# The front of a conformer, attention and PEER block: convolution sums in PSUM, projections in another order, part of the attention's elementwise work on ScalarE

## The chip, the cores and the metric

One NeuronCore of a Trainium2 chip runs the whole block as one program. The metric is the device time in microseconds of one execution; it is the median of several runs.

## The reference, cut to what matters

The block has 512 tokens (4 tiles of 128) of width 1024. Its front, which the change is about, is this:

```python
h = rmsnorm(x, norm1_g)
z = h @ w_in                      # 44 column chunks of 128: 16 for the conv, 8 q, 2 k, 2 v, 16 gates
u = z[..., :1024] * sigmoid(z[..., 1024:2048])              # GLU
u = depthwise_conv(u, width 31, centred) + dw_b             # 31 taps, each channel by itself
A = silu(layernorm(u)) @ w_pw
# windowed attention, 16 query heads, 4 key heads, |t-s| <= 128, ALiBi bias, one sink logit per head
p = exp(logits * scale + bias - m); o = (p @ v) / (p.sum() + exp(sink - m))
B = o @ w_o
x = x + (sigmoid(gate_A) * A + sigmoid(gate_B) * B) @ w_out
x = x + PEER(rmsnorm(x)); out = rmsnorm(x)                  # 128x128 experts, 8 heads, top 16
```

## The kernel before

Activations lie transposed: 128 channels on the partitions, 512 tokens along the free axis. Every fp32 product is made of three matmuls on a high and a low half (`mm3`, L61 to L66): L64 is high by high, L65 high by low, L66 low by high. A projection of one 128-column chunk is 8 contraction steps of three matmuls, so 24 matmuls of 128x512 into one PSUM bank (`proj`, L167). Its weights come by one 512 KB DMA of SP (`wraw`, 3 buffers); ACT makes the high half in two pieces (`whi`, L58, 4 buffers), and POOL the low half (`wlo`, L59).

The order of the front in the program text is: norm and transposes; GLU of channel chunks 0 and 1 (`glu`, L191: two projections `pa` and `pg`, a sigmoid on ACT, a product on DVE into `ub`); their convolution on DVE (`conv`, L203: one `TENSOR_SCALAR` for the first tap and 30 `SCALAR_TENSOR_TENSOR` per chunk, the two chunks of a pair taking turns, each adding into the tile `cv` in SBUF); k and v; the distance table; conv of pairs (2, 3), (4, 5) and (6, 7) with the q projections between them; the attention, 4 key groups by 4 query blocks (`attend`, L253); the LayerNorm over `cv`; 16 gate projections (`gate`, L240); then the projections by w_o (L350), w_pw (L388) and w_out, and the PEER part.

One `attend` has, for 4 heads, three score matmuls into a PSUM tile `s`, a DVE reduction that adds the bias and finds the maximum (L267), an exponential on ACT (L275), sums and a reciprocal on DVE, four normalisations on DVE (L282), transposes on PE (`pt`), a split into `ph` (ACT) and `pl` (DVE), and the product with v into `o`.

The order on each engine is not the order of the text. The tile framework schedules ahead of time, by program priority and its own estimates, and each engine then runs its list strictly in that order. What has no dependency on the conv is therefore already spread among its taps. PSUM has 8 banks: before, 2 for `mm` (all projections), 2 for `s`, 2 for `pt`, 1 each for `o` and `ln`.

Of the kernel before, what the change touches and what calls it, by code (L numbers as in the profile page):

```python
# [7 lines left out]
F32 = mybir.dt.float32  # L8
# [4 lines left out]
AF = mybir.ActivationFunctionType  # L13
OP = mybir.AluOpType
AX = mybir.AxisListType
PSUM = bass.MemoryType.PSUM

P = 128
S = 512
D = 1024  # L20
NT = S // P
KD = D // P
TAPS = 31
# [22 lines left out]
def encoder_block(ctx, tc, x, g1, w_in, taps, dwb, lng, lnb, w_pw, sink, w_o, w_out, g2, g2row,  # L46
# [71 lines left out]
    with ExitStack() as fc:  # L118
# [45 lines left out]
            POOL.dma_start(keyt, keys)  # L164
        hT = [(hT_hi[:, k, :], hT_lo[:, k, :]) for k in range(KD)]

        def proj(src, rhs, ws=None, lo_engine=POOL):  # L167
            ws = ws or weights(src, lo_engine)
            ps = psm.tile([P, S], F32, name="mm")
            mm3(ps, ws, rhs)  # L170
            return ps

# [4 lines left out]
        with ExitStack() as ac:  # L177
# [5 lines left out]
            dist = kvp.tile([P, 3 * P], F32, name="dist")  # L183
            aw = ac.enter_context(tc.tile_pool(name="aw", bufs=2))
            psa = ac.enter_context(tc.tile_pool(name="psa", bufs=2, space=PSUM))
            pso = ac.enter_context(tc.tile_pool(name="pso", bufs=1, space=PSUM))

            glup = ExitStack()
            gl = glup.enter_context(tc.tile_pool(name="gl", bufs=2))

            def glu(i):  # L191
                pa = proj(w_in[i], hT, first if i == 0 else None)
                pg = proj(w_in[8 + i], hT)
                sgm = gl.tile([P, S], F32, name="sgm")
                ACT.activation(sgm, pg, AF.Sigmoid)
                ub = gl.tile([P, S + 2 * PAD], F32, name="ub", bufs=4)
                POOL.memset(ub[:, :PAD], 0.0)
                POOL.memset(ub[:, PAD + S:], 0.0)
                with tc.high_priority():
                    DVE.tensor_tensor(ub[:, PAD:PAD + S], pa, sgm, op=OP.mult)  # L200
                return ub

            def conv(pair, ubs):  # L203
                for j in range(TAPS):
                    for i, ub in zip(pair, ubs):
                        acc = cv[:, i, :]
                        if j == 0:
                            DVE.tensor_scalar(acc, ub[:, :S], tapt[:, i, 0:1], vec["dwb"][:, i:i + 1],
                                              op0=OP.mult, op1=OP.add)
                        else:  # L210
                            DVE.scalar_tensor_tensor(acc, ub[:, j:j + S], tapt[:, i, j:j + 1], acc,  # L211
                                                     op0=OP.mult, op1=OP.add)

            conv((0, 1), [glu(0), glu(1)])
            for i in range(2):
                ps = proj(w_in[24 + i], hT)
                with tc.high_priority():
# [22 lines left out]
            def gate(i):  # L240
                ps = proj(w_in[28 + i], hT)
                ACT.activation(sg[i // KD][:, i % KD, :], ps, AF.Copy)
# [3 lines left out]
            def make_bias(g):  # L246
                bt = aw.tile([P, 4, 3 * P], F32, name="bias", bufs=1)
                for i in range(4):
                    slope = 2.0 ** (-8.0 * (4 * g + i + 1) / NH)
                    POOL.tensor_scalar(bt[:, i, :], dist, -8.0 * slope, None, op0=OP.mult)  # L250
                biases[g] = bt

            def attend(g, b):  # L253
                k0, k1 = max(0, b - 1), min(NT, b + 2)
                n = (k1 - k0) * P
                c0 = (k0 - (b - 1)) * P
                rows = slice(64 * (g % 2), 64 * (g % 2) + 64)
                gp = g // 2
                cols = slice(b * P, (b + 1) * P)
                L = aw.tile([P, 4, 3 * P], F32, name="L", bufs=3)  # L260
                m = sm.tile([P, 4], F32, name="m")
                for i in range(4):
                    s_ps = psa.tile([P, S], F32, name="s")
                    mm3(s_ps[:, :n], [(qh[rows, gp * 4 + i, cols], ql[rows, gp * 4 + i, cols])],
                        [(kh[rows, gp, k0 * P:k1 * P], kl[rows, gp, k0 * P:k1 * P])])
                    h = 4 * g + i
                    DVE.tensor_tensor_reduce(L[:, i, :n], s_ps[:, :n], biases[g][:, i, c0:c0 + n], 0.125,  # L267
                                             sinkt[:, h:h + 1], OP.add, OP.max, m[:, i:i + 1])
                nm = sm.tile([P, 4], F32, name="nm")
                DVE.tensor_scalar(nm, m, -1.0, None, op0=OP.mult)  # L270
                es = sm.tile([P, 4], F32, name="es")
                DVE.tensor_tensor(es, sinkt[:, 4 * g:4 * g + 4], m, op=OP.subtract)
                den = sm.tile([P, 4], F32, name="den")
                for i in range(4):
                    ACT.activation(L[:, i, :n], L[:, i, :n], AF.Exp, bias=nm[:, i:i + 1],  # L275
                                   accum_out=den[:, i:i + 1])
                ACT.activation(es, es, AF.Exp)
                DVE.tensor_tensor(den, den, es, op=OP.add)
                rd = sm.tile([P, 4], F32, name="rd")
                DVE.reciprocal(rd, den)  # L280
                for i in range(4):
                    DVE.tensor_scalar(L[:, i, :n], L[:, i, :n], rd[:, i:i + 1], None, op0=OP.mult)  # L282
                o_ps = pso.tile([P, 4, P], F32, name="o")
                for j in range(k1 - k0):
                    pt = psa.tile([P, 4, P], F32, name="pt", bufs=2)
                    for i in range(4):
                        PE.transpose(pt[:, i, :], L[:, i, j * P:(j + 1) * P], ident)
                    ph = aw.tile([P, S], F32R, name="ph")
                    pl = aw.tile([P, S], F32R, name="pl")
                    split(ph, pl, pt.rearrange("p a b -> p (a b)"), DVE)  # L290
                    vcols = slice(gp * P, (gp + 1) * P)
                    mm3(o_ps.rearrange("p a b -> p (a b)"),
                        [(vh[:, k0 + j, vcols], vl[:, k0 + j, vcols])], [(ph, pl)],
                        first=j == 0, last=j == k1 - k0 - 1)
                split(qh[rows, gp * 4:gp * 4 + 4, cols], ql[rows, gp * 4:gp * 4 + 4, cols], o_ps[rows], DVE)
# [5 lines left out]
            DVE.tensor_scalar(dtmp, dist, float(P), 1e32, op0=OP.is_gt, op1=OP.mult)  # L301
            DVE.tensor_tensor(dist, dist, dtmp, op=OP.add)

            conv((2, 3), [glu(2), glu(3)])
            for i in range(4):
                qproj(i)
            conv((4, 5), [glu(4), glu(5)])
            for i in range(4, 8):
                qproj(i)
            conv((6, 7), [glu(6), glu(7)])  # L310
            for g in range(4):
                make_bias(g)
                for b in range(NT):
                    attend(g, b)
            glup.close()
            lnp = ac.enter_context(tc.tile_pool(name="lnp", bufs=2))
            ac_hi, ac_lo = bigtile(), bigtile()
            mu_ps = pso.tile([P, S], F32, name="ln")
# [23 lines left out]
                sgf = sg[i].rearrange("p k s -> p (k s)")  # L342
                ACT.activation(sgf, sgf, AF.Sigmoid)

            for k in range(KD):
                gate(KD + k)
            sigmoid(1)
            for k in range(KD):
                gate(k)
            for j in range(KD):  # L350
                ps = proj(w_o[j], oT, lo_engine=DVE)
                DVE.tensor_tensor(sg[1][:, j, :], ps, sg[1][:, j, :], op=OP.mult)
# [80 lines left out]
    with ExitStack() as rc:  # L433
# [73 lines left out]
        with qc:  # L507
# [45 lines left out]
            for h in range(HP):  # L553
                scs = []
                for p in range(2):
                    n = 2 * h + p
# [251 lines left out]
```

## Time and profile before

| what | value |
|---|---|
| median of 3 runs | 1873.43 us (1873.26 to 1878.59) |
| the profiled execution | 1870.83 us, its span 1869.1 us |
| granted TensorE clock, mean | 0.979 |
| PE, PEld, DVE, ACT, POOL busy | 94%, 80%, 82%, 40%, 56% |
| first projection matmul | 15.57 us |
| conv taps on DVE | 30.5 to 286.3 us |
| first matmul by w_o, first by w_pw | 432.53 us, 477.33 us |

A time is read from the first instruction of the span. "PE busy" counts modelled ends of pipelined matmuls, so a full 20.00 in a 20 us window says only that PE never ran dry; the count of matmuls in a window says how much it did. A fast 128x512 matmul starts 0.227 us after the one before it, about 88 in 20 us.

### The profile page before, as it was taken

What the parts mean: (1) busy time and instruction counts of PE and PEld (TensorE: products, weight loads), DVE (VectorE), ACT (ScalarE), POOL (GpSimd) and SP (SyncE); (2) the same over time, 40 slices, a digit from 0 to 9 for tenths busy, and PEclk for the clock granted to TensorE, in tenths of its full rate; (3) what the DMA queues carried; (4) which work ended last, traced back from release to release, by engine and by line L of the source; (5) the groups of instructions that cost most, each with busy time, mean ns of one, the idle gap of its engine ahead of it and who ended that gap; (6) DMA issues with size and microseconds to landing.
All of it is one profiled execution on the core that took longest, in us unless ns stands there. A gap on an engine that the chain in (4) does not pass through costs nothing.

```text
span 1869.1 us, 25289 instructions
## 1 busy us (share of the span) xinstructions
PE 1751.3 (94%) x8873; PEld 1495.0 (80%) x8873; DVE 1536.5 (82%) x2649; ACT 753.2 (40%) x1329; POOL 1049.0 (56%) x757
## 2 busy tenths in 40 slices
PE   7878879999999986887899999999999999999998
PEld 5656656778887876776889899999999999999886
DVE  5999978854534999999798899998988977797874
ACT  4222325865224414554443333333333333333243
POOL 4544373231015525465535788788887888787611
PEclk9999889999999999999999999999999999999999
DMA  4122111034234202468866989898998888887972
GB/s 152 58 77 75 61 46 35 12 92 167 68 102 150 88 26 93 137 191 253 275 221 239 340 320 337 297 330 317 325 336 306 330 311 316 313 314 292 351 270 97
DMA packets 148943, 379.43 MB, mean 203 GB/s; under 512 B 11520, under 2 KB 63760, under 8 KB 148816
## 3 DMA queue, kind: packets, MB, share of 16 engines
q1 hardware_dynamic: 110832, 241.20, 37.2%
q0 software_dynamic: 37120, 134.52, 20.3%
q10 hardware_dynamic: 864, 2.10, 0.3%
q8 instruction: 69, 1.13, 0.2%
q14 instruction: 58, 0.48, 0.1%
HBM read 346.84 MB, written 30.93 MB: 202 GB/s over the span
## 4 chain that ended last, share of the span: by engine, by line
PE 40%; DVE 14%; DMA 5%; issue 2%; POOL 2%; ACT 1%; SPq 0%; POOLq 0%; DVEq 0%; ACTq 0%
PE acc L65 7%; PE acc L66 7%; PE acc L64 7%; PE hps L66 6%; PE hps L64 6%; PE hps L65 6%; DVE oi L594 1%; DVE ohi L596 1%; DVE olo L597 1%; DVE oj L595 1%; DVE vlo L59 1%; DMA row<-in_v_dram,eidx 1%; DMA vraw<-in_v_dram 1%; DVE ij L496 1%; POOL ulo L59 1%
## 5 line engine op out<-in xcount | busy, mean ns | idle before, releaser
L59 POOL TENSOR_TENSOR ulo<-uraw,uhi 128x512 fp32r<-128x512 f32 x256 | 423.8, 1671 | 279.7 <-ACT uhi L58 262.9
L64 PE MATMUL hps<-big,uhi 128*128 128x384 f32 x1024 | 350.9, 343 | 7.8 <-ACT hb L429 7.7
L66 PE MATMUL hps<-big,ulo 128*128 128x384 f32 x1024 | 350.2, 342 | 2.6 <-POOL ulo L59 2.6
L65 PE MATMUL hps<-big,uhi 128*128 128x384 f32 x1024 | 349.4, 341 | 0.0
L59 POOL TENSOR_TENSOR wlo<-wraw,whi 128x512 fp32r<-128x512 f32 x120 | 194.8, 1631 | 231.5 <-ACT whi L58 205.6
L65 PE MATMUL acc<-vlo,ph 128*128 128x512 f32 x768 | 300.2, 391 | 2.0 <-DVE vlo L59 2.0
L64 PE MATMUL acc<-vhi,ph 128*128 128x512 f32 x768 | 298.9, 390 | 1.2 <-ACT vhi L58 1.2
L66 PE MATMUL acc<-vhi,pl 128*128 128x512 f32 x768 | 299.6, 390 | 0.0
L64 PE MATMUL mm<-big,whi 128*128 128x512 f32 x544 | 224.2, 412 | 28.0 <-DVE ub L200 12.4
L58 ACT ACTIVATE uhi<-uraw 128x512 fp32r<-128x512 f32 x256 | 155.5, 629 | 206.7 <-DMA uraw<-in_ut_dram 83.9
L641 DVE SCALAR_TENSOR_TENSOR yacc<-row,dots,yacc 128x1024 f32<-128x1024 f32 x127 | 189.2, 1490 | 58.0 <-DMA row<-in_v_dram,eidx 57.7
L66 PE MATMUL mm<-big,wlo 128*128 128x512 f32 x544 | 220.2, 405 | 14.5 <-POOL wlo L59 14.4
L630 DVE SCALAR_TENSOR_TENSOR row<-row,h2tok 128x1024 f32<-128x1024 f32 x128 | 193.9, 1521 | 34.6 <-DMA row<-in_u_dram,eidx 33.9
L58 ACT ACTIVATE vhi<-vraw 128x1024 fp32r<-128x1024 f32 x128 | 135.0, 1055 | 212.3 <-DMA vraw<-in_v_dram 200.2
L65 PE MATMUL mm<-big,whi 128*128 128x512 f32 x544 | 220.0, 404 | 0.0
L211 DVE SCALAR_TENSOR_TENSOR cv<-ub,tapt,cv 128x512 f32<-128x512 f32 x240 | 212.1, 930 | 1.8
L58 ACT ACTIVATE whi<-wraw 128x512 fp32r<-128x512 f32 x152 | 94.7, 631 | 287.4 <-PE mm L65 169.7
L64 PEld LDWEIGHTS hps<-big,uhi 128*128 128x128 f32 x1024 | 195.1, 191 | 15.4 <-ACT hb L429 8.7
L623 POOL DMA_INDIRECT row<-in_v_dram,eidx x128 | 176.3, 1377 | 49.3 <-DVE yacc L641 20.3
L623 POOL DMA_INDIRECT row<-in_u_dram,eidx x128 | 182.9, 1429 | 33.1 <-issue 17.5
L65 PEld LDWEIGHTS hps<-big,uhi 128*128 128x128 f32 x1024 | 195.5, 191 | 4.1
L66 PEld LDWEIGHTS hps<-big,ulo 128*128 128x128 f32 x1024 | 194.8, 190 | 3.6 <-POOL ulo L59 3.6
(217 smaller groups left out, 3027.0 us busy)
## 6 DMA issues: line engine op xcount, KB each, us to landing
uraw<-in_ut_dram SPq DMA_DIRECT2D x128, 512.0 KB, 7.1
vraw<-in_v_dram SPq DMA_DIRECT2D x128, 512.0 KB, 5.5
gates_dram<-st SPq DMA_DIRECT2D x12, 2048.0 KB, 9.9
gt<-gates_dram SPq DMA_DIRECT2D x32, 768.0 KB, 7.0
wraw<-in_w_in_dram SPq DMA_DIRECT2D x44, 512.0 KB, 3.3
wraw<-in_w_query_dram SPq DMA_DIRECT2D x16, 512.0 KB, 3.4
oraw<-in_w_out_dram SPq DMA_DIRECT2D x16, 256.0 KB, 3.1
wraw<-in_w_o_dram SPq DMA_DIRECT2D x8, 512.0 KB, 3.8
```

The lines of the kernel that those rows point to most:

```text
L58: ACT.activation(hi, src, AF.Copy)
L59: lo_engine.tensor_tensor(lo, src, f(hi), op=OP.subtract)
L64: PE.matmul(ps, wh, mh, start=first and i == 0, stop=False)
L65: PE.matmul(ps, wh, ml, start=False, stop=False)
L66: PE.matmul(ps, wl, mh, start=False, stop=last and i == n - 1)
L211: DVE.scalar_tensor_tensor(acc, ub[:, j:j + S], tapt[:, i, j:j + 1], acc, op0=OP.mult, op1=OP.add)
L496: DVE.tensor_reduce(ij[t][:, s, hs, :].rearrange("p h k -> p (h k)"), oh.rearrange("p a h k -> p (h k) a"), AX.X, OP.add)
L594: DVE.tensor_tensor(prs(oi), iota8, row(0), op=OP.is_equal)
L595: DVE.tensor_tensor(prs(oj), iota8, row(1), op=OP.is_equal)
L623: POOL.indirect_dma_start(out=row, out_offset=None, in_=table, in_offset=bass.IndirectOffsetOnAxis(ap=eidx[:, c:c + 1], axis=0))
L630: DVE.scalar_tensor_tensor(row, row, 1.0, h2tok, op0=OP.mult, op1=OP.mult, accum_out=dots[:, c:c + 1])
L641: DVE.scalar_tensor_tensor(yacc, row, dots[:, c:c + 1], yacc, op0=OP.mult, op1=OP.add)
```

## The change

Four things are changed. The running sum of the convolution is kept in a PSUM tile (`ca`, two banks, pool `psc`), and only the last tap writes to `cv`. The GLU's two projections use the banks of `s` in place of those of `mm`. The order in the text is another: the GLU chunks 2 and 3 stand ahead of k and v, each later pair's GLU ahead of the conv in front of it, and 3, 6 and 2 of the gate projections stand between the channel pairs, 5 among the attention (`fill`), in the order B, A, B, A. In the attention, the bias tables are made by ACT in place of POOL, and two of each four normalisations by ACT in place of DVE. The banks of `o` and `ln` are opened only after those of `ca` are closed, so no `o` product can start while a conv runs.

```diff
-            pso = ac.enter_context(tc.tile_pool(name="pso", bufs=1, space=PSUM))
             glup = ExitStack()
+            psc = glup.enter_context(tc.tile_pool(name="psc", bufs=2, space=PSUM))
             def glu(i):
-                pa = proj(w_in[i], hT, first if i == 0 else None)
-                pg = proj(w_in[8 + i], hT)
+                pa = proj(w_in[i], hT, first if i == 0 else None, ps=psa.tile([P, S], F32, name="s"))
+                pg = proj(w_in[8 + i], hT, ps=psa.tile([P, S], F32, name="s"))
             def conv(pair, ubs):
+                accs = [psc.tile([P, S], F32, name="ca") for _ in pair]
                 for j in range(TAPS):
-                    for i, ub in zip(pair, ubs):
-                        acc = cv[:, i, :]
+                    for i, ub, acc in zip(pair, ubs, accs):
                         if j == 0:
                             DVE.tensor_scalar(acc, ub[:, :S], ...)
                         else:
-                            DVE.scalar_tensor_tensor(acc, ub[:, j:j + S], tapt[:, i, j:j + 1], acc,
-                                                     op0=OP.mult, op1=OP.add)
+                            DVE.scalar_tensor_tensor(cv[:, i, :] if j == TAPS - 1 else acc, ub[:, j:j + S],
+                                                     tapt[:, i, j:j + 1], acc, op0=OP.mult, op1=OP.add)
-            conv((0, 1), [glu(0), glu(1)])
+            ub01 = [glu(0), glu(1)]
+            conv((0, 1), ub01)
+            ub23 = [glu(2), glu(3)]
...
-                    POOL.tensor_scalar(bt[:, i, :], dist, -8.0 * slope, None, op0=OP.mult)
+                    ACT.activation(bt[:, i, :], dist, AF.Copy, scale=-8.0 * slope)
...
-                    DVE.tensor_scalar(L[:, i, :n], L[:, i, :n], rd[:, i:i + 1], None, op0=OP.mult)
+                    if i % 2:
+                        ACT.activation(L[:, i, :n], L[:, i, :n], AF.Copy, scale=rd[:, i:i + 1])
+                    else:
+                        DVE.tensor_scalar(L[:, i, :n], L[:, i, :n], rd[:, i:i + 1], None, op0=OP.mult)
...
-            conv((2, 3), [glu(2), glu(3)])
+            gates = [gate_of for k in range(KD) for gate_of in (KD + k, k)]
+            def fill(n):
+                for _ in range(n):
+                    gate(gates.pop(0))
             for i in range(4):
                 qproj(i)
-            conv((4, 5), [glu(4), glu(5)])
+            conv((2, 3), ub23)
+            ub45 = [glu(4), glu(5)]
             for i in range(4, 8):
                 qproj(i)
-            conv((6, 7), [glu(6), glu(7)])
+            fill(3)
+            conv((4, 5), ub45)
+            ub67 = [glu(6), glu(7)]
+            fill(6)
+            conv((6, 7), ub67)
+            fill(2)
+            glup.close()
+            pso = ac.enter_context(tc.tile_pool(name="pso", bufs=1, space=PSUM))
             for g in range(4):
                 make_bias(g)
                 for b in range(NT):
                     attend(g, b)
-            glup.close()
+                    if b == 1 or (g, b) == (0, 3):
+                        fill(1)
...
-            for k in range(KD):
-                gate(KD + k)
             sigmoid(1)
-            for k in range(KD):
-                gate(k)
```

Where instructions stand on DVE, in the conv of the second channel pair; `ql` is the low half of a q projection, `L` here a score block of the attention. Before:

```order
L211 SCALAR_TENSOR_TENSOR cv<-ub,tapt,cv 128x512 x8
L59 TENSOR_TENSOR ql<-mm,qh 128x512
L211 SCALAR_TENSOR_TENSOR cv<-ub,tapt,cv 128x512 x13
L267 ISA L,m<-s,bias,sinkt 128x256
L267 ISA m 128x1
L200 TENSOR_TENSOR ub<-mm,sgm 128x512
L211 SCALAR_TENSOR_TENSOR cv<-ub,tapt,cv 128x512
L208 TENSOR_SCALAR cv<-ub,tapt,dwb 128x512
```

And now, at the same q projections:

```order
L210 SCALAR_TENSOR_TENSOR ca<-ub,tapt,ca 128x512 x6
L59 TENSOR_TENSOR ql<-mm,qh 128x512
L210 SCALAR_TENSOR_TENSOR ca<-ub,tapt,ca 128x512 x15
L199 TENSOR_TENSOR ub<-s,sgm 128x512
L210 SCALAR_TENSOR_TENSOR ca<-ub,tapt,ca 128x512 x3
L210 SCALAR_TENSOR_TENSOR cv<-ub,tapt,ca 128x512
L210 SCALAR_TENSOR_TENSOR ca<-ub,tapt,ca 128x512
L207 TENSOR_SCALAR ca<-ub,tapt,dwb 128x512
```

The taps read and write `ca`, and the product that makes `ub` reads the bank `s`. No instruction of the attention stands among the taps now.

On ACT, about the GLU of the last channel pair and the first exponentials (`sgm` is the GLU's sigmoid, `sg` a stored gate, `den` the sum of the exponentials). Before:

```order
L58 ACTIVATE whi<-wraw 128x512 x3
L275 ACT_TABLE_LOAD
L275 ACTIVATE L,den<-L,nm 128x256
L195 ACT_TABLE_LOAD
L195 ACTIVATE sgm<-mm 128x512
L58 ACTIVATE whi<-wraw 128x512
L275 ACT_TABLE_LOAD
L275 ACTIVATE L,den<-L,nm 128x256 x3
L277 ACTIVATE es<-es 128x4
```

And now, behind all GLU sigmoids and eleven of the gates:

```order
L243 ACTIVATE sg_82<-mm 128x512
L58 ACTIVATE whi<-wraw 128x512 x2
L243 ACTIVATE sg_83<-mm 128x512
L276 ACT_TABLE_LOAD
L276 ACTIVATE L,den<-L,nm 128x256 x4
L278 ACTIVATE es<-es 128x4
L276 ACTIVATE L,den<-L,nm 128x384
L284 ACTIVATE L<-L,rd 128x256 x2
```

All eight sigmoids of the GLU and eleven gates come ahead of the first exponential, and each block has two normalisations (L284) on ACT.

On PE, at the end of the attention (`o` is the product with v, `mm<-big` a gate projection, `mm<-qh` one by w_o, `ln<-sq` the LayerNorm's variance). Before:

```order
L64 MATMUL o<-ph,vh 128x512
L65 MATMUL o<-pl,vh 128x512
L66 MATMUL o<-ph,vl 128x512
L65 MATMUL mm<-big,whi 128x512
L66 MATMUL mm<-big,wlo 128x512
L64 MATMUL mm<-big,whi 128x512
```

And now:

```order
L64 MATMUL o<-ph,vh 128x512
L65 MATMUL o<-pl,vh 128x512
L66 MATMUL o<-ph,vl 128x512
L346 MATMUL ln<-sq,ones 128x512 x4
L64 MATMUL mm<-qh,whi 128x512
L65 MATMUL mm<-ql,whi 128x512
L346 MATMUL ln<-sq,ones 128x512 x2
L66 MATMUL mm<-qh,wlo 128x512
```

Before, 113 gate matmuls follow the last `o`; now the variance and then 166 matmuls by w_o follow it, 26 of the 192 by w_o having come earlier.

## Rows read from the trace of the kernel before

**Rows 1.** Windows of 20 us in the conv stretch, all engines.
```profile
core 0: us, PE busy (x) PEld busy (x) DVE busy (x) ACT busy (x) POOL busy (x), PEclk, DMA share, GB/s
40.00:60.00 20.00, 15.13 (x59) 11.79 (x58) 19.82 (x24) 4.61 (x8) 7.36 (x5) 0.88 0.24 81
100.00:120.00 20.00, 13.26 (x51) 10.44 (x50) 19.72 (x25) 3.69 (x7) 6.17 (x4) 0.83 0.17 52
240.00:260.00 20.00, 6.11 (x20) 4.60 (x19) 20.00 (x31) 1.12 (x2) 20.00 (x4) 0.66 0.04 10
```

**Rows 2.** Windows of the conv stretch and of the attention, columns as above.
```profile
280.00:406.00 126.00, 124.63 (x581) 86.88 (x580) 108.05 (x298) 89.57 (x215) 34.48 (x25) 1.00 0.08 27
20.00:262.00 242.00, 197.69 (x786) 152.65 (x786) 231.38 (x292) 59.42 (x102) 124.80 (x75) 0.91 0.20 66
```

**Rows 3.** Waits, 20 to 262 us: total, times, longest.
```profile
PE mm L66 <- POOL wlo L59: 13.9, 1, 13.9
PE mm L64 <- DVE ub L200: 12.4, 4, 6.7
PE mm L64 <- DVE ql L59: 8.0, 5, 3.1
```

**Rows 4.** Conv taps by their line, POOL's low halves by tile: ns min/median/max.
```profile
L211 DVE SCALAR_TENSOR_TENSOR cv<-ub,tapt,cv x240: 733/747/1789, 30.5 to 286.3; 128x512 f32<-128x512 f32 x120
L59 POOL TENSOR_TENSOR wlo<-wraw,whi x88: 1257/1460/21874, 13.0 to 426.2; 128x512 fp32r<-128x512 f32 x88
```

**Rows 5.** Timeline of DVE and POOL: start, length, instruction, count.
```profile
231.34 23.94 DVE L211 SCALAR_TENSOR_TENSOR cv<-ub,tapt,cv 128x512 f32<-128x512 f32 x36
...
234.52 21.87 POOL L59 TENSOR_TENSOR wlo<-wraw,whi 128x512 fp32r<-128x512 f32 x1 [7.74 <-ACT whi L58]
```

**Rows 6.** DVE instructions that read PSUM, and ACT's square into PSUM or SBUF.
```profile
L104 DVE SCALAR_TENSOR_TENSOR big<-mm,g,big x8: 743/747/751, 15.5 to 20.2; 128x512 fp32r<-128x512 f32 x8
...
L59 DVE TENSOR_TENSOR pl<-pt,ph x40: 669/681/692, 255.2 to 405.4; 128x512 fp32r<-128x512 f32 x40
...
L86 ACT ACTIVATE xn<-xt x4: 1040/1049/1058, 6.1 to 10.4; 128x1024 f32<-128x1024 f32 x4
...
L86 ACT ACTIVATE junk<-x x4: 1023/1029/1029, 549.7 to 567.9; 128x1024 f32<-128x1024 f32 x4
```

**Rows 7.** Timeline of PE at three places.
```profile
18.21 0.39 PE L66 MATMUL mm<-big,wlo 128*128 128x512 f32 x1
...
27.75 0.39 PE L66 MATMUL mm<-big,wlo 128*128 128x512 f32 x1
29.18 0.50 PE L64 MATMUL mm<-big,whi 128*128 128x512 f32 x1 [1.04 <-ACT sgm L195]
...
57.00 0.63 PE L65 MATMUL mm<-big,whi 128*128 128x512 f32 x1
...
432.53 0.40 PE L64 MATMUL mm<-qh,whi 128*128 128x512 f32 x1
...
477.33 0.39 PE L64 MATMUL mm<-big,whi 128*128 128x512 f32 x1
```

**Rows 8.** Groups in the attention, 280 to 406 us: busy, mean ns.
```profile
L65 PE MATMUL mm<-big,whi 128*128 128x512 f32 x48 | 21.0, 438 | 0.0
...
L328 PE MATMUL ln<-sq,ones 128*128 128x512 f32 x16 | 8.6, 618 | 0.0
...
L275 ACT ACTIVATE L<-L,nm 128x384 f32<-128x384 f32 x28 | 16.9, 610 | 1.3 <-DVE nm L270 1.1
L275 ACT ACTIVATE L<-L,nm 128x256 f32<-128x256 f32 x28 | 13.9, 501 | 2.0 <-DVE nm L270 1.9
...
L343 ACT ACTIVATE sg<-sg 128x4096 f32<-128x4096 f32 x1 | 3.6, 3625 | 0.0
...
L282 DVE TENSOR_SCALAR L<-L,rd 128x384 f32<-128x384 f32 x32 | 16.1, 553 | 0.1
```

**Rows 9.** LayerNorm's reciprocal, 0 to 600 us: busy, mean ns.
```profile
L331 DVE RECIPROCAL rs<-rs 128x512 f32<-128x512 f32 x1 | 3.4, 3350 | 0.0
```

More of the change, by code (lines that the diff above doesn't have):

```diff
@@ L165, in encoder_block, with proj @@
         hT = [(hT_hi[:, k, :], hT_lo[:, k, :]) for k in range(KD)]
-        def proj(src, rhs, ws=None, lo_engine=POOL):
+        def proj(src, rhs, ws=None, lo_engine=POOL, ps=None):
             ws = ws or weights(src, lo_engine)
-            ps = psm.tile([P, S], F32, name="mm")
+            ps = psm.tile([P, S], F32, name="mm") if ps is None else ps
             mm3(ps, ws, rhs)
```

## The prediction

> **What bounds the kernel now.** I read the windows of the front first, since the change ends there: everything behind the first matmul by w_pw stands as it stood. From 20 to 262 us DVE is busy 231.4 of 242 us [rows 2], and in single windows all of 20.00, while PE does 51 or 59 matmuls where a full window holds 88, and 20 in the window at 240 us [rows 1]. So the conv on DVE sets the pace there and PE waits for it. The waits then say through what: PE waits 13.9 us in one piece for POOL's `wlo`, 12.4 us for the GLU product `ub`, 8.0 us for `ql` [rows 3]. Next, why DVE is that long. A tap takes 747 ns in the median but up to 1789; POOL's low half is 1257 at best and once 21874 [rows 4]. The timeline shows both sides of it: 36 taps run in 23.94 us, 0.665 us each, and in that very stretch one `wlo` of POOL lasts 21.87 us [rows 5]. A tap reads two tensors in SBUF, as does POOL's subtraction; one holds the other up. DVE instructions that read one tensor from PSUM show nothing of it: 40 of `pl` lie between 669 and 692 ns, 8 of L104 between 743 and 751 [rows 6].
>
> The attention is another regime: from 280 to 406 us PE is busy 124.6 of 126 us at clock 1.00, with DVE at 108 and ACT at 90 [rows 2]. There PE is the bound.
>
> The starved PE pays twice: after an idle stretch its matmuls are slower for a while (0.63 us at 57 us, where others show 0.39 [rows 7]), and the mean granted clock of the conv stretch is 0.91, of its worst window 0.66 [rows 1, 2], so for a part of that time it is at the lower of its two levels.
>
> **The change part by part.** PE's work is the same matmuls before and after, so I follow PE's list up to the first matmul by w_pw, which started at 477.33 us [rows 7].
>
> *Stage A, up to the first score.* Now 39 projections stand there: 16 for the GLU, 4 for k and v, 8 q, 11 gates. From 18.21 to 27.75 us lie 42 fast matmuls [rows 7], 0.227 us each, 5.45 us a projection. The first two end at 27.98; the other 37 take 201.7 us. Where two GLU chunks follow each other, the second waits for a bank, 1.2 us at 29.18 [rows 7]; five such places, since k, q and gates use other banks: 6.0 us. The transposes of v add about 1. Stage A ends at 236.7 us, if PE never starves.
>
> Does DVE let it? 240 taps at 0.665 us are 159.6 us; 8 first taps, 8 `ub`, 12 `kl`, `vl`, `ql` and three distance instructions are 18; about 6 go in waits for the first GLU chunks, and DVE starts at 29.2. That is 213 us, and by its list, where 47 taps follow the last `ub` (PE gives it at 193.1 us), about 226. So PE is the bound by some 10 us at the end and 24 in sum; a tap may take up to 0.766 us (53 + 240 times p = 236.7) before PE waits. The `ql` between 6 or 7 taps come every 5.3 us on DVE, just below PE's 5.45. A tap that writes PSUM is not in the trace. From below: `pl`, no scalar operand, 681 ns; from above: a tap that waits out POOL, 1789 ns [rows 4, 6]. L104 is the same instruction with one input in PSUM and takes 747, as the median tap does; and ACT writes 1024 columns to PSUM in 1029 ns and to SBUF in 1049 [rows 6]. I take 0.665 us from start to start. POOL, no longer held up, needs two low halves, 1257 ns each at best [rows 4], in the 5.45 us of a projection.
>
> [...] Here L104 with a PSUM input and the tap without one show 747 ns both. [...]
>
> *Stage B, the attention.* In 280 to 406 us stand 581 records, 144 of them gate matmuls (48 of each of three lines [rows 8]); these are 32.7 us at 0.227, which leaves 93.3 us for 437 of attention and LayerNorm, 0.2135 us each. All 16 blocks have 192 scores, 160 transposes and 120 products with v, and 16 LayerNorm matmuls are recorded twice (x16 for 8 of them [rows 8]): 504 records, 107.6 us. With 5 gates (27.3) and the 26 early matmuls by w_o (6.1) this is 141.0 us. Two things are added: 3 us for the first block, whose chain of scores, exponentials and transposes has only 20 gate matmuls to hide behind, and 3 us for ACT, below. Nothing of it could start earlier, because 8 gates stand in front of it on PE, and DVE does its first score only after the last tap. Stage B ends at 383.7.
>
> ACT takes over 32 normalisations and 12 of the bias instructions there. The nearest row is the exponential, 610 ns on 384 columns and 501 on 256 [rows 8]: 17.8 us and 7.3. The old 89.6 us held 14 of 16 blocks (56 exponentials of 64), so 102 for all; the second sigmoid adds 3.6 [rows 8]. Together 131 us beside PE's 141, table loads of the second sigmoid not counted. It is hidden, but barely, hence the 3. DVE loses the same 32, at 553 ns on 384 columns [rows 8], and has room. POOL loses the biases; it was idle there.
>
> *Stage C.* The other 166 matmuls by w_o take 38.7 us at the 0.2333 us of their own stage (192 in 432.53 to 477.33 [rows 7]). The variance's last matmuls now come after the last `o`; in DVE's list the reciprocal of 3350 ns [rows 9] and seven products stand ahead of what empties w_o's banks, so PE waits for banks: 4 us in all. The first matmul by w_pw comes at 383.7 + 38.7 + 4 = 426.4 us, 50.9 earlier than 477.33.
>
> The rest moves along unchanged: 1870.83 - 50.9 = 1819.9 us of the profiled execution. The median of the runs shown is 2.6 us above that execution, so 1822.5; I say 1823.
>
> **The rivals.**
>
> *ACT binds the attention.* For it: over 131 of 141 us in a strict order, with each block's chain crossing from PE to DVE to ACT and back. Against it: in the old attention PE's waits were small with ACT at 90 of 126. If each of the 16 blocks costs 1.5 us more, 24 us are lost: 1847. [...] Here the row of DVE is 553 ns on 384 columns, waits for POOL in it, against about 610 on ACT, which does not decide between them.
>
> *A tap in PSUM is much longer (the slower side).* Each tap reads the sum that the tap two places before has just written, now through PSUM, and no row shows that round trip. If it is p from start to start, stage A ends at 53 + 240p. It eats the whole gain from p = 0.98 on (288 us) and is worth 1.1 us, for instance, 317 us, 80 later than forecast: 1903. Speaking for it: nothing in the trace excludes it, and the far bound of 1789 ns would give far more. Against: L104 and ACT's square.
>
> *The blocking stays.* A tap still reads `ub` and its coefficients from SBUF. If DVE then needs the 231.4 us of its old conv stretch [rows 2] from 29.2 us on, and the 6 us of early waits, stage A ends at 267 us, 30 late: 1853. Against it: 40 `pl`, all with one SBUF input, and no long one among them.
>
> *More than forecast.* Without POOL's and DVE's mutual holds the attention's records cost less than 0.2135 us: 10 us less would be 1813, and 1805 if the stalls of stages B and C vanish too.
>
> **How the numbers follow.** The forecast, a gain of 36 to 64 us, has 0.63: 1809 to 1838 is its own range. ACT as the bound 0.18 (1838 to 1858), more than forecast 0.05, blocking stays (around 1853) 0.06, the longer tap 0.08, of which a little ends near the old time. About 0.3% (5.6 us) can be told from no change. Faster: 0.90; within it 0.02; slower 0.08. The range from 1804 to 1850 leaves out the last two cases and part of the second.
>
> **What would show it.** Right: taps of about 750 ns without a tail at 1700, `wlo` at 1.3 us, 88 matmuls in each window of 20 us from 40 to 230 us at clock 1.00, the first score near 237 us, the first matmul by w_pw near 426. Wrong: DVE full and PE at 60 in these windows (taps long or blocked), ACT over 19 of 20 us between 240 and 380 with PE waiting for `ph`, `qh` or normalised `L`, or PE idle for several microseconds behind the last `o`.

## The result, and the profile after

The changed kernel takes 1832.4 us (median of 4 runs, 1827.3 to 1836.5), the kernel before 1876.0 (4 runs): a ratio of 0.9764, 95% interval 0.9729 to 0.9798. The forecast was 1823, with 1804 to 1850 as its range. The profiled execution has 1832.5 us, 38.3 less than that of before.

First the taps and GpSimd's low halves, by tile: count, ns min/median/max, first and last start. They answer to [rows 4].

```profile
L210 DVE SCALAR_TENSOR_TENSOR ca<-ub,tapt,ca x232: 737/752/756, 36.9 to 233.6; 128x512 f32<-128x512 f32 x116
L210 DVE SCALAR_TENSOR_TENSOR cv<-ub,tapt,ca x8: 740/743/748, 73.3 to 234.4; 128x512 f32<-128x512 f32 x8
...
L207 DVE TENSOR_SCALAR ca<-ub,tapt,dwb x8: 806/810/815, 36.1 to 202.2; 128x512 f32<-128x512 f32 x8
...
L59 POOL TENSOR_TENSOR wlo<-wraw,whi x88: 1257/1292/1482, 13.2 to 293.0; 128x512 fp32r<-128x512 f32 x88
```

The tails are gone: no `SCALAR_TENSOR_TENSOR` tap above 756 ns where one took 1789, no low half above 1482 where one took 21874. The median tap is 5 ns longer than it was. The eight first taps (L207, a `TENSOR_SCALAR`) did get longer with their result in PSUM, 810 ns in the median; before, this was one of them:

```profile
46.84 0.53 DVE L208 TENSOR_SCALAR cv<-ub,tapt,dwb 128x512 f32<-128x512 f32 x1
```

Next the windows (columns as in [rows 1]), which answer to [rows 1, 2].

```profile
40.00:60.00 20.00, 17.92 (x78) 14.21 (x77) 17.73 (x27) 5.39 (x9) 8.67 (x8) 1.00 0.23 79
100.00:120.00 20.00, 20.00 (x90) 16.56 (x89) 18.58 (x30) 7.72 (x15) 10.06 (x8) 1.00 0.31 104
220.00:240.00 20.00, 20.00 (x90) 16.57 (x89) 14.66 (x21) 6.36 (x11) 9.88 (x8) 1.00 0.27 94
240.00:260.00 20.00, 20.00 (x96) 14.46 (x94) 10.45 (x34) 13.73 (x34) 5.25 (x4) 1.00 0.16 54
280.00:360.00 80.00, 80.00 (x361) 54.40 (x360) 51.73 (x167) 64.23 (x147) 3.17 (x3) 1.00 0.08 27
20.00:236.00 216.00, 209.68 (x912) 171.56 (x913) 184.68 (x273) 64.87 (x112) 98.90 (x85) 0.99 0.27 91
...
360.00:380.00 20.00, 17.64 (x90) 12.71 (x89) 14.30 (x41) 19.49 (x54) 0.00 (x0) 1.00 0.00 0
380.00:400.00 20.00, 18.66 (x66) 11.85 (x66) 15.10 (x18) 16.84 (x27) 10.55 (x8) 1.00 0.60 182
400.00:420.00 20.00, 16.91 (x66) 12.76 (x66) 14.51 (x24) 11.47 (x19) 0.00 (x0) 0.91 0.52 183
```

TensorE does 90 matmuls at 100 us where it did 51, at clock 1.00 instead of 0.83, and VectorE is busy 184.7 of 216 us instead of 231.4 of 242. The last three rows are new. From 360 us ScalarE is all but full (19.49 of 20 us), and about the end of the attention and behind it TensorE does 66 matmuls in a window. Before, a window behind the attention was this:

```profile
400.00:420.00 20.00, 19.80 (x90) 15.86 (x90) 5.18 (x12) 11.26 (x20) 11.45 (x10) 1.00 0.53 158
```

TensorE's waits from 20 to 262 us (total, times, longest; [rows 3]):

```profile
PE s L64 <- ACT sgm L194: 5.2, 5, 1.0
PE s L64 <- DVE big L104: 3.3, 1, 3.3
```

The waits for `wlo`, `ub` and `ql` are gone; the second line is new. Four places of TensorE's timeline (start, length; [rows 7]): the last transposes of x, the first projection, the first score, the first matmul by w_pw.

```profile
16.52 1.31 PE L102 MATMUL mm<-ident,xn 128*128 128x128 f32 x8 [1.97 <-DVE big L104]
21.13 0.79 PE L64 MATMUL s<-big,whi 128*128 128x512 f32 x1 [3.29 <-DVE big L104]
...
243.38 0.38 PE L64 MATMUL s<-kh,qh 64*128 64x256 f32 x1
...
434.12 0.39 PE L64 MATMUL mm<-big,whi 128*128 128x512 f32 x1
```

So the first w_pw matmul comes 43.2 us earlier than before; 38.3 of these are left at the end of the profiled execution. From there to the end the statements did not change. In the profiled executions of this study that stretch took between 1390 and 1401 us (1393.5 before, 1398.4 after), in no relation to the edits; the 4.9 us lie within this scatter. The comparisons below therefore rest on the first w_pw matmul and on the ratio with its interval, and not on one time.

### The profile page after: what moved, and what is told of

Read it like the earlier page. It is cut to its first block, busy times and chain, and to the rows that moved or that the text cites. A ratio compares the mean times of both kernels' runs of the same rounds, so it can differ in the third digit from the quotient of the medians.

```text
span 1830.7 us, 25268 instructions
## 1 busy us (share of the span) xinstructions
PE 1747.4 (95%) x8873; PEld 1495.6 (82%) x8873; DVE 1469.2 (80%) x2617; ACT 768.0 (42%) x1371; POOL 969.6 (53%) x741
## 4 chain that ended last, share of the span: by engine, by line
PE 41%; DVE 16%; DMA 4%; issue 2%; POOL 1%; ACT 1%; SPq 0%; DVEq 0%; POOLq 0%; ACTq 0%
PE acc L65 7%; PE acc L66 7%; PE acc L64 7%; PE hps L64 6%; PE hps L66 6%; PE hps L65 6%; DVE oi L608 2%; DVE ohi L610 2%; DMA row<-in_v_dram,eidx 2%; DVE olo L611 2%; DVE oj L609 2%; DVE vlo L59 1%; DMA gt<-gates_dram 1%; DVE ij L510 1%; DMA vraw<-in_v_dram 1%
## 5 line engine op out<-in xcount | busy, mean ns | idle before, releaser
L59 POOL TENSOR_TENSOR wlo<-wraw,whi 128x512 fp32r<-128x512 f32 x120 | 156.4, 1306 | 200.0 <-ACT whi L58 198.4
L644 DVE SCALAR_TENSOR_TENSOR row<-row,h2tok 128x1024 f32<-128x1024 f32 x128 | 203.1, 1593 | 37.4 <-DMA row<-in_u_dram,eidx 36.7
L655 DVE SCALAR_TENSOR_TENSOR yacc<-row,dots,yacc 128x1024 f32<-128x1024 f32 x127 | 177.4, 1397 | 64.8 <-DMA row<-in_v_dram,eidx 64.4
L637 POOL DMA_INDIRECT row<-in_v_dram,eidx x128 | 163.1, 1274 | 50.6 <-DVE yacc L655 22.4
L59 DVE TENSOR_TENSOR vlo<-vraw,vhi 128x1024 fp32r<-128x1024 f32 x128 | 175.5, 1372 | 15.6 <-ACT vhi L58 14.2
L65 PEld LDWEIGHTS acc<-vlo,ph 128*128 128x128 f32 x768 | 144.1, 188 | 32.1 <-DVE vlo L59 5.8
L66 PEld LDWEIGHTS acc<-vhi,pl 128*128 128x128 f32 x768 | 144.2, 188 | 30.9 <-DVE pl L59 0.3
L64 PEld LDWEIGHTS acc<-vhi,ph 128*128 128x128 f32 x768 | 144.1, 188 | 30.0 <-ACT vhi L58 2.0
```

The lines of the kernel that those rows point to most:

```text
L59: lo_engine.tensor_tensor(lo, src, f(hi), op=OP.subtract)
L64: PE.matmul(ps, wh, mh, start=first and i == 0, stop=False)
L65: PE.matmul(ps, wh, ml, start=False, stop=False)
L66: PE.matmul(ps, wl, mh, start=False, stop=last and i == n - 1)
L637: POOL.indirect_dma_start(out=row, out_offset=None, in_=table, in_offset=bass.IndirectOffsetOnAxis(ap=eidx[:, c:c + 1], axis=0))
L644: DVE.scalar_tensor_tensor(row, row, 1.0, h2tok, op0=OP.mult, op1=OP.mult, accum_out=dots[:, c:c + 1])
```

## The experiments

**The sums in SBUF again, nothing else.** Only the first sum stays in PSUM, so that the banks are held as before.

```
-  scalar_tensor_tensor(cv[:, i, :] if j == TAPS - 1 else acc, ub[:, j:j + S], ..., acc, ...)
+  scalar_tensor_tensor(cv[:, i, :], ub[:, j:j + S], ..., acc if j == 1 else cv[:, i, :], ...)
```

> The changed kernel with the conv sums from the second tap on in SBUF again; TensorE's and ScalarE's lists are word for word those of the changed kernel. Theory (a tap that reads two tensors from SBUF and GpSimd's subtraction hold each other up): taps of 0.75 us in the median with a tail above 1.6 us, low halves `wlo` up to 20 us, TensorE waiting in the conv stretch, first score about 270 us instead of 243.4, and the whole at 1850 to 1870 us. Rival (the new order of the projections makes the gain, where the sums stand does not matter): no tail, first score within 3 us of 243.4, 1827 to 1838 us.

Measured: 1879.5 us, ratio to the kernel before 1.0058 (1.0036 to 1.0079): 0.6% slower than before, and worse than the theory's own numbers. First score 275.2, first w_pw 482.7. Its taps and low halves by tile, and three windows:

```profile
L210 DVE SCALAR_TENSOR_TENSOR cv<-ub,tapt,cv x232: 734/742/1879, 37.5 to 285.4; 128x512 f32<-128x512 f32 x116
...
L59 POOL TENSOR_TENSOR wlo<-wraw,whi x88: 1259/1352/5887, 12.9 to 339.8; 128x512 fp32r<-128x512 f32 x88
```

```profile
60.00:80.00 20.00, 15.63 (x63) 12.47 (x62) 20.00 (x27) 3.52 (x6) 8.12 (x4) 0.91 0.16 54
140.00:160.00 20.00, 14.42 (x56) 11.14 (x55) 19.86 (x26) 3.64 (x6) 6.22 (x9) 0.91 0.20 61
280.00:300.00 20.00, 13.42 (x42) 10.10 (x43) 11.50 (x32) 4.45 (x16) 0.00 (x0) 0.57 0.02 8
```

With one operand moved the tail is back, 72 of 248 taps last over 1 us, VectorE is full and TensorE starves. A low half stood still for at most 5.9 us, not 20. TensorE's and ScalarE's lists are the same here; VectorE and GpSimd have the same instructions, some of them in another order (at most 12 taps stand elsewhere at one place). So the 48.6 us between 482.7 and 434.1 are the place of the sums and what that reordering does. The taps' durations say which is the larger: the 72 long taps together exceed 0.815 us, the longest tap of the changed kernel, by 58.6 us. The rest of the change by itself is a loss: all attention now stands behind the conv, and when that is late nothing runs beside it (the third row: 42 matmuls, clock 0.57).

**The statement order of before, with the sums in PSUM.**

```
+  psc = glup.enter_context(tc.tile_pool(name="psc", bufs=2, space=PSUM))     # in the kernel before
-  vps2, pt: psa.tile(..., name="pt", bufs=2)
+  vps2: psa.tile(..., name="s");  pt: psa.tile(..., name="pt", bufs=1);  "ln" in a pool opened after the conv
```

> The kernel before with its own order of the projections and only the conv sums moved to PSUM; for the two banks one buffer of `pt` is given up and LayerNorm's bank is opened after the conv. Theory (the hold between taps and GpSimd is the larger part of the loss): VectorE's conv stretch shrinks by about 30 us, TensorE's waits for `wlo`, `ub` and `ql` go, gain of 20 to 35 us less 2 to 5 for the missing `pt`: 1843 to 1856. Rival (what counted was that nothing else stood in TensorE's list to fill its waits): gain under 10 us, 1863 to 1878.

Measured: 1825.6 us, ratio 0.9766 (0.9739 to 0.9794), the changed kernel's ratio, without a projection moved by hand and without ScalarE's normalisations; the gain is larger than even the theory had it. First w_pw at 426.0, 8 us before the changed kernel's. It isn't the old list with another operand: from the same statements the scheduler now sets 435 projection matmuls in a row ahead of most of the attention, where it had mixed the two.

**All normalisations on VectorE, biases on GpSimd.**

```
-  if i % 2: ACT.activation(L..., AF.Copy, scale=rd...)
-  else: DVE.tensor_scalar(L..., rd...)
+  DVE.tensor_scalar(L..., rd...)
-  ACT.activation(bt..., dist, AF.Copy, scale=-8.0 * slope)
+  POOL.tensor_scalar(bt..., dist, -8.0 * slope, None, op0=OP.mult)
```

> The changed kernel with all 64 normalisations on VectorE and the biases on GpSimd, as before the change. Theory (the attention is bound by TensorE and its chain over both engines, neither ScalarE nor VectorE is full): first w_pw matmul within 3 us of 433.9, 1828 to 1837 us. First rival (ScalarE sets the attention's pace, so its load cost something): first w_pw 5 us or more earlier, 1827 us or less. Second rival (VectorE would have been the bound, so the move bought something): first w_pw 8 us or more later, 1840 us or more.

Measured: 1837.4 us, ratio 0.9851 (0.9820 to 0.9881); first w_pw 441.8, 7.7 later. The first theory falls; the numbers stop a little short of the second rival's. From the first score to the end of the last `o` it takes 147.2 us against 139.8. But what that rival gives as the reason isn't there: VectorE was busy 99.3 of 140 us from 240 to 380. Its normalisations, with the biases, and those of the changed kernel (busy, mean ns, 240 to 385 us):

```profile
L288 PE MATMUL pt<-ident,L 128*128 128x128 f32 x156 | 24.8, 281 | 2.6 <-DVE L L283 2.5
...
L283 DVE TENSOR_SCALAR L<-L,rd 128x384 f32<-128x384 f32 x32 | 15.6, 549 | 0.2
...
L251 POOL TENSOR_SCALAR bias<-dist 128x384 f32<-128x384 f32 x12 | 14.3, 1195 | 46.5 <-DVE m L268 45.8
...
L283 DVE TENSOR_SCALAR L<-L,rd 128x256 f32<-128x256 f32 x32 | 9.9, 363 | 0.1
```

```profile
L291 PE MATMUL pt<-ident,L 128*128 128x128 f32 x160 | 24.0, 276 | 0.4 <-DVE pl L59 0.4
...
L284 ACT ACTIVATE L<-L,rd 128x384 f32<-128x384 f32 x16 | 9.0, 606 | 0.1
...
L284 ACT ACTIVATE L<-L,rd 128x256 f32<-128x256 f32 x16 | 7.2, 501 | 1.0 <-DVE rd L281 1.0
L286 DVE TENSOR_SCALAR L<-L,rd 128x384 f32<-128x384 f32 x16 | 7.1, 480 | 0.2
L251 ACT ACTIVATE bias<-dist 128x384 f32<-128x384 f32 x12 | 5.6, 517 | 0.0
L286 DVE TENSOR_SCALAR L<-L,rd 128x256 f32<-128x256 f32 x16 | 4.9, 350 | 0.2
```

A block's four normalisations of 384 columns take four times 549 ns in a row, or two of 606 beside two of 480. With all of them on VectorE, TensorE's transposes (L288) wait 2.5 us for normalised `L`; in the changed kernel (L291) they don't. From the end of a block's reciprocal to the end of its last normalisation it is 2.35 us in the mean of the 16 blocks here, and 1.86 in the changed kernel, 7.8 us less in sum. Blocks overlap, so this sum need not be the gain, but the step did get shorter. Whether the normalisations or the biases made the 7.7 us, the last runs decide, in the old order.

**The first GLU chunk in the banks of `mm`, then the chunks in turn.**

```
-  pa = proj(..., ps=psa.tile([P, S], F32, name="s"));  pg likewise
+  ps=psa.tile([P, S], F32, name="s") if i else None         # first run; "if i % 2" in the second
```

> The changed kernel with the first GLU chunk's two projections in the banks of `mm`, where the kernel before had them, and not in those of `s`. Theory (the banks of `s` were those of the transposes of x, so the first projection waited for the last of these): first projection near 15.6 us instead of 21.1, first score near 237 instead of 243.4, first w_pw near 428 and a gain of 5 to 7 us: 1825 to 1828. Rival (the delay is hidden by VectorE's chain of taps or by later stalls): first score within 2 us of 243.4, 1830 to 1835.

> The changed kernel with GLU chunks 0, 2, 4, 6 in the banks of `mm` and 1, 3, 5, 7 in those of `s`, so that of two chunks that follow each other the second needs no bank of the first. Theory (the waits of 1 us for `sgm` at such places are TensorE's own loss, as is the late start): first projection near 16 us, first score 231 to 234 us, first w_pw near 424 against 434.1 of the changed kernel and 429.1 with the first chunk alone moved; ratio to the kernel before 0.969 to 0.973. Rival (VectorE's taps end at 230 in any case and now set the end of the conv stretch): first score at 237 to 239, first w_pw 428 to 430, ratio 0.974 to 0.978.

Measured: for the first chunk alone 1822.5 us, ratio 0.9763 (0.9726 to 0.9799), first projection 16.0, first score 237.9, first w_pw 429.1. In turn: 1821.6 us, ratio 0.9736 (0.9712 to 0.9761), 15.5, 231.9 and 423.8. The marks follow the theory both times: 5 us for the late start, 5 to 6 more for the waits for `sgm`. The ratios can't confirm that: the first is the changed kernel's, 5 us being inside the interval, and the second's interval overlaps the changed kernel's. VectorE's last tap ends at 225.3 in the second run, 6 us before the first score: it is still not the bound.

**LayerNorm's statistics ahead of the last group.**

```
 for g in range(4):
+    if g == 3: (mean, variance, square root, reciprocal: moved here from behind the loop)
     for b in range(NT): attend(g, b)
```

> The same banks in turn, and LayerNorm's mean, variance and reciprocal stand ahead of the attention's last group instead of behind it. Theory (TensorE's loss behind the last `o` is VectorE's late reciprocal and products, queued ahead of what empties w_o's banks): from the last `o` to the first w_pw 40 to 43 us instead of 51, first w_pw 8 to 11 us earlier than without this, ratio 0.963 to 0.969. Rival (the statistics lengthen the attention by what the tail saves, since its chain runs over the same two engines): first w_pw within 3 us of the kernel with banks in turn alone, same ratio.

Measured: 1824.8 us, ratio 0.9752 (0.9728 to 0.9777), the interval overlapping that of banks in turn alone. Behind the last `o` 40.7 us as the theory has it, against 52.1 without; but the last `o` ends at 387.2 instead of 371.7, and the first w_pw comes at 427.9, 4 us later. So the rival is right, and in this execution by a little more than its 3 us. The tail is real, and moved this way it costs at least as much in the attention as it saves. What it is, VectorE's timeline of the changed kernel shows:

```profile
391.39 3.35 DVE L349 RECIPROCAL rs<-rs 128x512 f32<-128x512 f32 x1 [4.74 <-ACT rs L348]
394.77 0.69 DVE L366 TENSOR_TENSOR sg<-mm,sg 128x512 f32<-128x512 f32 x1
395.38 6.14 DVE L351 TENSOR_TENSOR cv<-cv,rs 128x512 f32<-128x512 f32 x7
401.44 1.28 DVE L59 TENSOR_TENSOR big<-act,big 128x512 fp32r<-128x512 f32 x2
402.64 0.68 DVE L351 TENSOR_TENSOR cv<-cv,rs 128x512 f32<-128x512 f32 x1
403.25 1.28 DVE L366 TENSOR_TENSOR sg<-mm,sg 128x512 f32<-128x512 f32 x2
```

L366 empties a bank of w_o. From the first of them to the next it is 8.5 us, filled with LayerNorm; TensorE waits 4.0 us for it (1.3 and 2.7) and then runs a stretch at a lower clock: 0.92 and 0.74 in the two windows of 5 us from 400 us on, 0.50 from 405 to 407.

**The order of before, banks in turn, without and with the split normalisations.** The bank edit above in the kernel with the old order; then, in the second, the lines that the third experiment took out.

> The kernel before in its own statement order with the sums in PSUM, one buffer of `pt`, and GLU chunks in the banks of `mm` and `s` in turn. Theory (seven waits of 1.0 us for `sgm` are all that TensorE still loses in its conv stretch): first w_pw 419 to 421 instead of 426.0, ratio 0.971 to 0.975. Rival (VectorE, at 18 to 19 of 20 us, is the bound there): first w_pw 424 to 427, ratio 0.975 to 0.979.

> The kernel of the run above with every second normalisation and the biases on ScalarE. Theory (with 16 gate projections left to stand among the attention, TensorE has other work while a block's chain runs over VectorE and ScalarE, so where the normalisations run does not matter): first w_pw and time within 2 us of the run above. Rival (the move shortens the attention in any order, as it did by 8 us in the new one): first w_pw 5 us or more earlier, ratio lower by 0.003 or more.

Measured: without, 1820.1 us, ratio 0.9738 (0.9708 to 0.9768), first w_pw 425.9: the waits for `sgm` are gone, but the first w_pw stays where it was. The theory's 419 to 421 is missed, and the mark falls where the rival has it, 424 to 427, though the ratio lies in the theory's range. The taps end at 227.3, though, instead of 231.6, and the last `o` comes at 384.0 instead of 381.8; so the rival's reason, VectorE full with taps, is not it either: the lead is lost in the attention. There TensorE's waits come to 7.2 us from 230 to 440 us, against 1.5 without the bank edit, and its clock is 0.83 in the window from 300 us and 0.91 in that from 380, where it was 1.00. With the split, 1811.4 us, ratio 0.9680 (0.9656 to 0.9703), first w_pw 417.7: 8.2 us for it here too, as its rival says, 16 gate projections or not.

**Which part of the split, and one more bank.** Three edits of the kernel just told: the biases back on GpSimd; `if i % 2` replaced by all four on ScalarE; a second buffer of `pt` in the conv's banks.

> The fastest kernel so far (statement order of before, sums in PSUM, GLU banks in turn, every second normalisation and the biases on ScalarE; first w_pw at 417.7 us, ratio 0.968), with the biases alone back on GpSimd. Theory (the 8 us came from the biases: a group's bias has one buffer, and four writes of 1.19 us on GpSimd after its last use stand in front of the next group's scores, against 0.51 us on ScalarE): first w_pw 423 to 426, ratio 0.972 to 0.975. Rival (they came from the normalisations: a block's four run two by two on two engines): first w_pw within 2 us of 417.7, ratio 0.966 to 0.970.

> The same fastest kernel with all four normalisations of a block on ScalarE. Theory (VectorE is relieved and ScalarE has room, so load decides: more relief, more gain): first w_pw 412 to 417.7, ratio 0.965 to 0.968. Rival (what counts is that the four run on two engines side by side; with one engine alone the chain of a block is as long as it was, and ScalarE at 116 of 140 us gets 18 us more): first w_pw 423 us or later, ratio 0.972 or more.

> The same fastest kernel, with the conv's two banks given to LayerNorm and to a second buffer of `pt` as soon as the last tap is done. Theory (with one `pt` the next transposes wait for both halves of the split of the one before; a second one takes these waits away): first w_pw 412 to 416, ratio 0.964 to 0.967. Rival (TensorE has gate projections to do meanwhile, 0.2 us of waits for `pt` are left in it): first w_pw within 2 us of 417.7, ratio 0.967 to 0.970.

Measured: biases on GpSimd 1808.5 us, ratio 0.9669 (0.9644 to 0.9695), first w_pw 415.2, as the rival has it (its 417.7 give or take 2 missed by 0.5, towards faster): in this order the biases are worth nothing, the normalisations all. All four on ScalarE 1827.3 us, ratio 0.9741 (0.9711 to 0.9770), first w_pw 436.0: the rival again, and all but the ratio with all four on VectorE (0.9738). The step from a block's reciprocal to its last normalisation takes 2.43 us in the mean with all four on VectorE, 2.03 and 2.09 with two on each engine (biases on ScalarE and on GpSimd), 3.27 with all four on ScalarE. Windows of that last run:

```profile
320.00:340.00 20.00, 18.62 (x87) 12.82 (x86) 10.82 (x36) 18.51 (x45) 0.00 (x0) 0.97 0.00 1
340.00:360.00 20.00, 18.73 (x54) 13.52 (x54) 8.65 (x30) 12.54 (x33) 0.00 (x0) 0.50 0.00 1
360.00:380.00 20.00, 17.82 (x56) 12.12 (x56) 7.08 (x17) 12.74 (x31) 5.03 (x4) 0.59 0.11 30
```

ScalarE fills 18.5 of 20 us, TensorE waits here and there (1.2 us in sum from 320 to 345 us), and then its clock stands at 0.50 for a whole window, with 54 matmuls in place of 87. This execution has the lowest mean clock of the six (0.975; the others 0.978 to 0.988), but its 1827.5 us is no more than their median, and no trace shows whether the others have such a window. So how much of the 436.0 is the longer step, how much the full ScalarE and how much the clock is not shown. That all four on one engine lose against two and two is: the ratio, from all six, lies apart from the other two. The second `pt` brought the last `o` forward to 361.1, but the first w_pw to 420.6 only, 2.9 later; ratio 0.9711 (0.9685 to 0.9737). Its theory falls, and the rival's 2 us are missed too: between the last `o` and the first matmul by w_o, at 375.4, now stand 64 matmuls of gate projections that had run beside the attention.

The kernel with the biases on GpSimd has the lowest ratio of all. Its interval lies below the changed kernel's and overlaps that of the same kernel with the biases on ScalarE. Its windows:

```profile
40.00:60.00 20.00, 20.00 (x90) 16.55 (x89) 19.17 (x30) 6.61 (x12) 9.07 (x8) 1.00 0.25 81
100.00:120.00 20.00, 20.00 (x90) 16.57 (x89) 18.76 (x30) 5.88 (x10) 9.96 (x8) 1.00 0.29 96
...
380.00:400.00 20.00, 20.00 (x88) 16.22 (x87) 9.71 (x13) 12.17 (x17) 11.50 (x8) 1.00 0.85 298
400.00:420.00 20.00, 20.00 (x88) 16.26 (x87) 6.64 (x10) 4.43 (x7) 0.00 (x0) 1.00 0.36 117
20.00:228.00 208.00, 208.00 (x921) 170.81 (x920) 183.39 (x281) 68.84 (x111) 104.51 (x89) 1.00 0.30 97
```

TensorE is busy in all of the conv stretch (208.0 of 208 us), and behind the attention the tail is gone: LayerNorm's matmuls end at 280.7 us, early in the attention, where the changed kernel has them from 334.9 to 389.1, and gate projections run beside the attention up to 363 us, where the changed kernel's end at 335.

## Why the prediction was right, and where it was not

*The mechanism was right.* Taps whose sum stands in PSUM and GpSimd's subtractions don't hold each other up (taps of 756 ns at most, low halves of 1482), and that carries the gain: with the sums back in SBUF, and TensorE's and ScalarE's lists as they were, all 43.2 us at the first w_pw are lost and 5.4 more; with the sums in PSUM, the old statement order gains as much as the new one. The rival of the blocking that stays is out (no such tap above 756 ns), and so is that of the longer tap: a tap takes 752 ns here and 747 to 750 in the other runs with sums in PSUM, against 747 before and 742 in the run with SBUF sums, and from start to start 0.658 us, where the forecast took 0.665. So no price of the bank shows in these taps. It does in the first tap of each chunk, 810 ns against 542 in the median before; that is 2 us in the whole conv, on an engine that is not the bound. Nor did the first score, 243.4 where 236.7 was forecast, come late through VectorE: its last tap was done 8 us before.

*Stage A, 236.7 forecast, 243.4 measured.* The step that failed is "the first two end at 27.98", read from the old list. The change also puts the GLU's projections in the banks of `s`, and the first of them now waits for the last transposes of x, with the clock at 0.50 from 20 to 25 us; the first projection moved from 15.57 to 21.13. The first chunk alone put back gives 5.5 of the 6.7 us. The five waits of 1 us at `sgm` were in the forecast and were there.

*Stage B, 147.0 forecast, 139.8 measured.* Two steps failed. One only moves time to the next stage: I counted all of LayerNorm's variance here, and 12 records of it, 5.7 us, came behind the last `o`. TensorE's timeline there:

```profile
382.80 0.40 PE L66 MATMUL o<-ph,vl 128*128 128x512 f32 x1
383.04 3.73 PE L346 MATMUL ln<-sq,ones 128*128 128x512 f32 x8
...
387.08 1.98 PE L346 MATMUL ln<-sq,ones 128*128 128x512 f32 x4
```

The other is the sign of "3 us for ACT". I counted ScalarE's busy time against TensorE's and took a loss, while a step of a block's chain got shorter by running on two engines (1.86 us in the mean against 2.35): with the normalisations on VectorE the stage takes 147.2 and the first w_pw comes 7.7 later. The rival that ScalarE binds is out for half of them as far as the stage goes, though one of its signs is there near the end: from 360 to 380 us ScalarE is busy 19.49 us and TensorE 17.64, and TensorE's waits for `ph` come to 1.2 us. For all of them, ratio 0.9741 against 0.9680, it is right in kind. The single instruction on 384 columns is the faster one on VectorE (480 ns there, 606 on ScalarE), but that does not settle it for the block: half of them on ScalarE were worth 8.2 us in the old order.

*Stage C, 42.7 forecast, 50.9 measured.* The stall for banks was there and of its size, 4.0 us. What the sum lacked are the 5.7 us of the variance, two more matmuls by w_o (168 behind the last `o`, not 166), and some 2 us at the lower clock (0.74 from 405 to 410 us) behind the waits (50.9 less 39.2 for 168 matmuls, 4.0 and 5.7).

The three stages miss by 6.7 - 7.2 + 8.2 = 7.7 us, and with the variance's 5.7 us counted where it came by 6.7 - 1.5 + 2.5. Another 4.9 were lost behind the first w_pw, in its scatter. Less the 2.7 by which the forecast put the median too far above the profiled execution, these are the 9.9 us from 1822.5 to 1832.4.

*What the prediction did not see* is that the moves by hand were worth nothing or less. I had counted 11 gates in stage A and 5 among the attention as filling what VectorE left open; but once no tap is held up, TensorE is near full in either order (209.7 of 216 us here, 204.6 of 212 in the old one), and the scheduler puts gates there by itself: of the 384 gate matmuls 229 run before the last tap here, and 232 in the old order with banks in turn and the split. One difference behind the conv is where LayerNorm's matmuls stand, late here and early there; why the scheduler sets them so is not shown. With banks in turn and the split in both, the old order reaches the first w_pw at 417.7 and the new one at 423.8 (ratios 0.9680 and 0.9736, intervals apart). These two differ in the banks of `pt` as well, one in the old order and two in the new, so the 6 us are not the order's alone for certain.

Not settled: why the second `pt` and the earlier end of the taps were lost again inside the attention. Each edit gives another list there, and no two of these lists differ in one thing alone.

## What to carry to other kernels

When an instruction's durations have a tail while its minimum is fixed, look for the engine that is busy in the same stretch and take away the shared operand (here: the running sum into PSUM, and none of the taps over 1 us where 72 of 248 were) before moving work about. Where a chain crosses engines, shorten a step of independent instructions by giving two engines a part each (here 8.2 us at the first w_pw for two and two normalisations in the old order); busy shares don't show what that is worth, in either direction. Before filler work is moved by hand, see what the scheduler does once the hold is gone: here it filled the conv stretch with as many gate matmuls by itself (232, against 229 by hand).

## What the runs showed of the hardware

- With TensorE's and ScalarE's lists unchanged, and VectorE's and GpSimd's nearly so, the place of one operand decides whether 72 of 248 taps last over 1 us or none.
- A result in PSUM in place of SBUF made the `TENSOR_SCALAR` of 128x512 longer, 810 ns against 542 in the median; the `SCALAR_TENSOR_TENSOR` that reads and writes its sum there stayed at 747 to 752 ns, against 742 to 747.
- In windows of 1 us of the first 570 us TensorE's clock reads 1.00 or 0.50, and something between only at a change from one to the other: 39 windows at 0.50 before, 8 in the changed kernel. On TensorE a wait of 2.7 us was followed by windows of 5 us at clock 0.92 and 0.74; in the run with all normalisations on ScalarE, waits of at most 0.7 us, 4.7 in sum from 335 to 385 us, went with a whole window of 20 us at 0.50. In the changed kernel 2.4 us of idle time from 360 to 380 us went with a clock of 1.00.
- Executions of one kernel differ in TensorE's mean clock and in time: the old order with banks in turn took 1815.8 us at 0.988 and 1833.6 at 0.978. The two need not go together: with the second `pt` it was 1822.0 us at 0.988 and 1817.8 at 0.984. The first difference is as large as most of the edits here.
